# A list scheduler that models two DMA queues and chooses orders by their mean end over late transfers, in a tuned 8-core hybrid block

## The chip, the cores and the metric

The kernel runs on all 8 cores of one Trainium2 chip, as one launch. Each core takes 4096 of the 32768 tokens. The cores don't exchange data, so the time of a run is the span of its slowest core, in microseconds of device time. There is a slower state, in which the cores of one die show a lower granted TensorE clock and the run is some per cent longer.

## The reference, cut to what matters

```python
h = rmsnorm(x, norm1_g)
p = h @ w_in                              # B, C, x~ (512 each) | u, v (512 each)
y_a = b_gate * causal_depthwise_conv(c_gate * xc, conv_w)
y_b = u * (spatial_gating(layernorm(v), w_s) + b_s)     # 128x128 per head, masked
y = concat([rmsnorm(y_a, g_conv), rmsnorm(y_b, g_gmlp)])
x = x + y @ w_out
a = relu(rmsnorm(x, norm2_g) @ w_up)
x = x + (a * a) @ w_down
return rmsnorm(x, final_g)
```

Here D is 1024 and the hidden width 4096. Each core works through 8 tiles of 512 tokens. The first stage (everything up to `y @ w_out`) takes the tiles one by one. After it comes the channel mixer, in four groups of two tiles.

## The kernel before

The program is not written in the order in which it runs. Every instruction is recorded as an operation with its inputs, and a list scheduler places the operations on five in-order queues: TensorE, ScalarE, VectorE, the gpsimd queue and the sync queue. The last two only issue transfers here, apart from little else. The order that it finds is fixed in the program. In the traces read here each queue keeps that order and waits for what hasn't arrived (8.60 us on ScalarE in the case told below).

```python
def schedule(self, phys, rounds=8):
    ...
    for _ in range(rounds + 1):
        order = self.place([op for op, _ in base], phys)   # forward: times in a model
        est = max(o.finish for o in order)
        if best is None or est < best[0]:
            best = (est, order, ...)
        self.push(order, est)                              # backward: new keys
```

In `place` a transfer is modelled by one queue that serves all transfers one after the other, whoever issues them:

```python
if op.dma_key is not None:
    dma_free = max(dma_free, st + op.occ) + op.nbytes / dma_rate     # 290e3 bytes per us
    op.finish = dma_free + dma_lat + op.margin                       # dma_lat = 2.0
else:
    op.finish = st + op.dur - op.occ + occ
```

`rstd` turns a sum of squares into the factor of a norm by a logarithm and an exponential, both on ScalarE. `stats` squares a tile in four quarters, on ScalarE too. The loads at the start are chained: each weight load (gpsimd queue, casting from f32) and each quarter of a tile (sync queue) is issued only when the load three places earlier in the list has landed.

```python
def rstd(out_ap, bank, n, writes, in_ap=None, reads=None):
    act(out_ap, bank[:, 0:n] ..., AF.Ln, ...)
    act(out_ap, out_ap, AF.Exp, writes, writes, n=n, scale=-0.5)

def stats(src, q, n, ones, rows=2, first=False):
    for j in range(0, n, 2):
        act(q[:, j:j + 2, :], src[:, j:j + 2, :], AF.Square, ...)
    ...

def wload(dst, src, keys, name, nbytes):
    landed = [("landed",) + name]
    dma("pool", dst, src, gate[-3], keys + landed, ("w",) + name, nbytes, key=first())
    gate.append(landed)
...
for k in (0, 4):
    wload(WU[:, k:k + 4, :], ...)           # two loads of 1 MB
for j in range(2):
    wload(WO[:, 4 * j:4 * j + 4, :], ...)   # two loads of 2 MB
load_x(2, gate)                             # third tile: X_72, four quarters of 512 KB
```

The third tile is called X_72 in the trace; its squares are XQ_80. The norm factors are the tiles RS_77 and RS_79, the normalised branches YN, and the output weights WO. PREP are two buffers in which the weights of the channel mixer are combined, RING the six slots that hold them in use, and RA and RB the residual with the result. `load_w` combines some of the down slots in the ring itself:

```python
def load_w(n):
    s, i = wslot(), plan[n]
    if n < 32 and 16 <= i < 24:
        combine(RING[s], ws(i), wdn_d, ...)    # loads f32 from wdn, adds, stores
    else:
        dma("sp", RING[s][:, :, :, :], ws(i), ...)
```

Of the kernel before, what the change touches and what calls it, by code (L numbers as in the profile page):

```python
# [23 lines left out]
KB = 1024  # L24

ENGS = ("pe", "act", "dve", "pool", "sp")


class Op:
# [6 lines left out]
class Bank:  # L36


    def __init__(self, log):
        self.ops, self.left, self.phys = [], 0, None  # L40
        log.append(self)
# [20 lines left out]

def real(x):
    return x.ap() if isinstance(x, Late) else x


class Sched:
# [41 lines left out]
        self.ops.append(op)  # L109
        return op  # L110

    def schedule(self, phys, rounds=8):


        base = [(op, op.deps) for op in self.ops]
        best = None
        for _ in range(rounds + 1):
            for op, deps in base:
                op.deps = deps
                for b in op.banks:  # L120
                    b.left = len(b.ops)
            order = self.place([op for op, _ in base], phys)
            est = max(o.finish for o in order)
            if best is None or est < best[0]:
                best = (est, order, [(o, o.deps) for o in order],
                        [(o.opens, o.opens.phys) for o in order if o.opens is not None],
                        {o: (o.start, o.finish) for o in order})
            self.push(order, est)
        self.est_total, self.ops = best[:2]
        for o, deps in best[2]:  # L130
            o.deps = deps
            o.start, o.finish = best[4][o]
        for b, p in best[3]:
            b.phys = p
        self.by_eng = {e: [o for o in self.ops if o.eng == e] for e in ENGS}

    def push(self, order, est, lat=0.12, dma_lat=2.0, dma_rate=290e3):

        left = {o: 0 for o in order}
        for o in order:  # L140
            o.late = est
            for d in o.deps:
                left[d] += 1
        ready = {e: [] for e in ENGS}
        for o in order:
            if not left[o]:
                ready[o.eng].append(o)
        t_free = {e: est for e in ENGS}
        dma_free = est

        def dur(o):
            return o.dur if o.dma_key is None else o.occ + o.nbytes / dma_rate + dma_lat + 2 * o.margin
        while True:
            best = None
            for e in ENGS:
                if not ready[e]:
                    continue
                horizon = min(t_free[e], max(o.late - dur(o) + o.occ for o in ready[e]))
                o = max((o for o in ready[e] if o.late - dur(o) + o.occ >= horizon), key=lambda o: (o.start, o.idx))
                if best is None or (horizon, o.idx) > best[0]:  # L160
                    best = ((horizon, o.idx), o)
            if best is None:
                return
            (end, _), o = best
            ready[o.eng].remove(o)
            if o.dma_key is not None:
                dma_free = min(dma_free, o.late - dma_lat - 2 * o.margin) - o.nbytes / dma_rate
                end = min(end, dma_free)
            t_free[o.eng] = end - o.occ
            if not o.fixed:  # L170
                o.key = t_free[o.eng]
            for d in o.deps:
                d.late = min(d.late, t_free[o.eng] - lat)
                left[d] -= 1
                if not left[d]:
                    ready[d.eng].append(d)

    def place(self, ops, phys, lat=0.12, dma_lat=2.0, dma_rate=290e3):
        free = [[t, 0.0, []] for t in phys]
        for op in ops:  # L180
            op.succs = []
            op.npred = len(op.deps)
            op.ready_t = 0.0
        for op in ops:
            for d in op.deps:
                d.succs.append(op)
        ready = {e: [] for e in ENGS}
        for op in ops:
            if op.npred == 0:
                ready[op.eng].append(op)  # L190
        t_free = {e: 0.0 for e in ENGS}
        dma_free = 0.0
        cold = 3.4
        order = []
        while True:
            best = None
            for e in ENGS:
                lst = ready[e]
                if not lst:
                    continue  # L200
                soon = min((f[1] for f in free), default=1e9)

                def ready_at(o):
                    return o.ready_t if o.opens is None else max(o.ready_t, soon)
                horizon = max(t_free[e], min(ready_at(o) for o in lst))
                if horizon >= 1e9:
                    continue
                op = min((o for o in lst if ready_at(o) <= horizon), key=lambda o: (o.key, o.idx))
                if best is None or (horizon, op.idx) < best[0]:
                    best = ((horizon, op.idx), op)  # L210
            if best is None:
                break
            (st, _), op = best
            ready[op.eng].remove(op)
            if op.opens is not None:
                f = min(free, key=lambda f: f[1])
                free.remove(f)
                op.opens.phys = f[0]
                op.deps = op.deps + f[2]
            op.start = st  # L220
            occ = op.occ
            if op.eng == "pe":

                if st - t_free["pe"] > 3.0:
                    cold = 3.4
                if cold > 0:
                    occ *= 2
                    cold -= occ
            t_free[op.eng] = st + occ
            if op.dma_key is not None:  # L230
                dma_free = max(dma_free, st + op.occ) + op.nbytes / dma_rate
                op.finish = dma_free + dma_lat + op.margin
            else:
                op.finish = st + op.dur - op.occ + occ
            order.append(op)
            for b in op.banks:
                b.left -= 1
                if b.left == 0:
                    last = [o for o in b.ops if o.eng != "pe"]
                    free.append([b.phys, max(o.finish for o in b.ops) + lat, last])  # L240
            for sc in op.succs:
                sc.npred -= 1
                sc.ready_t = max(sc.ready_t, op.finish + lat)
                if sc.npred == 0:
                    ready[sc.eng].append(sc)
        assert len(order) == len(ops)
        return order

    def resolve(self):
# [70 lines left out]
def build_program():  # L320
    nc = bass.Bass("TRN2", target_bir_lowering=False)
    S = Sched()
# [21 lines left out]
    with es:  # L344
        base = (nc.sbuf_base + 1023) // 1024 * 1024
# [14 lines left out]
        o = 6  # L360
# [54 lines left out]
        banks = []  # L415
# [13 lines left out]
        def act(out, in_, func, reads, writes, n=MT, **kw):  # L429
            aps = sum(1 for v in kw.values() if not isinstance(v, (int, float)))  # L430
            S.add("act", lambda e: e.activation(out=out, in_=real(in_), func=func, **kw), reads=reads, writes=writes,  # L431
                  occ=(n / 1.2 + 200 + 70 * aps) / 1000, banks=[in_.bank] if isinstance(in_, Late) else [])

        def dve(fn, reads, writes, n=MT, rate=1, src=None):
            S.add("dve", fn, reads=reads, writes=writes, occ=(n / rate + 151) / 960,
                  banks=[src.bank] if isinstance(src, Late) else [])

        def tt(out, in0, in1, op, reads, writes, n=MT, rate=1):
            dve(lambda e: e.tensor_tensor(out=out, in0=real(in0), in1=in1, op=op), reads, writes, n, rate, in0)  # L439
# [176 lines left out]
        def ws(i):  # L616
            return ws_d[i].rearrange("p (a k n) -> p a k n", a=7, k=4)

        def prep(i, n):
            combine(PREP[n % 2], ws(i), wup_d if i < 16 else wdn_d, (i, ("pl", n % 2), ("ps", n % 2)), WO.keys(4) if n < 2 else [], 5.0)  # L620
# [7 lines left out]
        def wslot():  # L628
            return nxt("ring", RG)

        def load_w(n):
            s, i = wslot(), plan[n]
            if n < 32 and 16 <= i < 24:
                combine(RING[s], ws(i), wdn_d, (i, ("fl", s), ("fs", s)), [], 5.0)
            else:
                dma("sp", RING[s][:, :, :, :], ws(i), [("ws", i)], RING[s].keys(0, 7), ("wl", s), 2 * 128 * 3584,
                    margin=2.0)
            return s
# [258 lines left out]
        def prep_some(m):  # L897
            if m >= 1 and pos["prep"] < 24:
                n = pos["prep"]
                prep(n if n < 16 else n + 8, n)  # L900
                pos["prep"] += 1

        pos["prep"] = 0
# [165 lines left out]
```

## Time and profile before

The three runs that came with the kernel have a median of 1244.42 us (1244.34 to 1245.89).

| before, profiled run | core 7 (slowest) | mean of 8 cores |
|---|---|---|
| span | 1244.9 us | 1240.0 us |
| first product of the first convolution | 18.9 us | 18.0 us |
| TensorE's wait for YN at the first output projection | 0.0 us | 0.0 us |
| last product of the channel mixer ends | 1227.9 us | 1223.3 us |
| from there to the end | 17.0 us | 16.7 us |

The first fence is from the page of the profile, core 7: its first line, the busy times of the engines, and the shares of the chain that ended last, by engine and by line.

```profile
span 1244.9 us, 18564 instructions; the slowest of 8 cores (1235.7 to 1244.9 us)
PE 1209.6 (97%) x5880; PEld 548.5 (44%) x5880; DVE 893.4 (72%) x1377; ACT 530.4 (43%) x905; POOL 86.0 (7%) x146
PE 93%; DMA 5%; DVE 1%; issue 0%; SPq 0%; DVEq 0%; POOLq 0%
PE PS L424 93%; DMA WSB_109<-bsf 2%; DMA X_74<-xT 1%; DMA X_73<-xT 1%; DMA WV<-wv 1%; DMA WCXB_53<-wcxb 1%; DVE RA L439 0%; DVE RB L439 0%; SPq L450 0%; DVE WU L446 0%; DVEq L344 0%; DVE FSQ_102 L439 0%; DVE FSQ_101 L439 0%; DVE Z L439 0%; DVEq L284 0%
```

The second is one line of the chain of waits in order of time, same core. Its columns are start, length, and what held the chain.

```profile
68.66 1158.35 PE PS L424 x5536
```

From 68.66 to 1227.01 us nothing but TensorE's own work is on the chain. The order of instructions holds 5468 products of 512 columns; at the 0.2157 us between two of them, and with the smaller ones, that is 1200.85 us of work (an estimate from these durations). So a core that ends its last product at 1227.9 us has lost 27.0 us over all, and the rest of its span is the tail. Part of the loss is half clock: after some waits the trace records a granted TensorE clock of 0.5 for some us, and products of 512 columns then start every 0.427 us and not every 0.2157 (33.63 us, core 7).

### The profile page before, as it was taken

What the parts mean: (1) busy time and instruction counts of PE and PEld (TensorE: products, weight loads), DVE (VectorE), ACT (ScalarE), POOL (GpSimd) and SP (SyncE); (2) the same over time, 40 slices, a digit from 0 to 9 for tenths busy, and PEclk for the clock granted to TensorE, in tenths of its full rate; (3) what the DMA queues carried; (4) which work ended last, traced back from release to release, by engine and by line L of the source; (5) the groups of instructions that cost most, each with busy time, mean ns of one, the idle gap of its engine ahead of it and who ended that gap; (6) DMA issues with size and microseconds to landing.
All of it is one profiled execution on the core that took longest, in us unless ns stands there. A gap on an engine that the chain in (4) does not pass through costs nothing.

```text
span 1244.9 us, 18564 instructions; the slowest of 8 cores (1235.7 to 1244.9 us)
## 1 busy us (share of the span) xinstructions
PE 1209.6 (97%) x5880; PEld 548.5 (44%) x5880; DVE 893.4 (72%) x1377; ACT 530.4 (43%) x905; POOL 86.0 (7%) x146
## 2 busy tenths in 40 slices
PE   5899999999999999999999999999999999999994
PEld 3444444444444444444444444444444444444442
DVE  2778687877878887658759737767846876855746
ACT  4544655536554356026127205317405406503524
POOL 0100000000001011000101200000110000110000
PEclk9899999999999999999999999999999999999998
DMA  8968688596675869975577764576984645985423
GB/s 185 171 148 232 167 228 231 148 245 175 179 220 153 279 213 207 237 266 176 169 260 228 262 212 162 211 237 177 295 272 148 216 165 182 279 271 177 149 90 135
DMA packets 55183, 253.81 MB, mean 204 GB/s; under 512 B 6192, under 2 KB 6320, under 8 KB 54832
## 3 DMA queue, kind: packets, MB, share of 16 engines
q1 hardware_dynamic: 35152, 180.27, 42.8%
q0 software_dynamic: 19936, 72.36, 25.3%
q8 instruction: 49, 0.80, 0.3%
q14 instruction: 46, 0.38, 0.1%
HBM read 211.71 MB, written 65.01 MB: 222 GB/s over the span
## 4 chain that ended last, share of the span: by engine, by line
PE 93%; DMA 5%; DVE 1%; issue 0%; SPq 0%; DVEq 0%; POOLq 0%
PE PS L424 93%; DMA WSB_109<-bsf 2%; DMA X_74<-xT 1%; DMA X_73<-xT 1%; DMA WV<-wv 1%; DMA WCXB_53<-wcxb 1%; DVE RA L439 0%; DVE RB L439 0%; SPq L450 0%; DVE WU L446 0%; DVEq L344 0%; DVE FSQ_102 L439 0%; DVE FSQ_101 L439 0%; DVE Z L439 0%; DVEq L284 0%
## 5 line engine op out<-in xcount | busy, mean ns | idle before, releaser
L439 DVE TENSOR_TENSOR RB<-PS,RB 128x512 f32<-128x512 f32 x128 | 87.4, 690 | 91.4 <-PE PS L424 88.9
L424 PE MATMUL PS<-YN,WO 128*128 128x512 f16 x512 | 113.8, 379 | 0.0
L439 DVE TENSOR_TENSOR RA<-PS,RA 128x512 f32<-128x512 f32 x96 | 66.1, 690 | 60.6 <-PE PS L424 59.2
L439 DVE TENSOR_TENSOR A_89<-A_89 128x512 bf16<-128x512 bf16 (+1 forms) x192 | 94.5, 508 | 8.2 <-ACT A_89 L431 3.6
L431 ACT ACTIVATE SN_92<-PS 128x512 f32<-128x512 f32 x63 | 37.4, 595 | 106.5 <-PE PS L424 104.7
L424 PEld LDWEIGHTS PS<-YN,WO 128*128 128x128 f16 x512 | 50.1, 98 | 60.4
L424 PE MATMUL PS<-A_89,RING_83 128*128 128x512 bf16 x308 | 76.1, 379 | 0.0
L424 PE MATMUL PS<-A_89,RING_85 128*128 128x512 bf16 x308 | 76.1, 379 | 0.0
L424 PE MATMUL PS<-A_89,RING_86 128*128 128x512 bf16 x308 | 75.8, 379 | 0.0
L424 PE MATMUL PS<-A_89,RING_84 128*128 128x512 bf16 x308 | 75.5, 379 | 0.0
L424 PE MATMUL PS<-H_96,RING_87 128*128 128x512 f16 x308 | 75.1, 379 | 0.0
L424 PE MATMUL PS<-H_96,RING_83 128*128 128x512 f16 x308 | 74.5, 379 | 0.0
L424 PE MATMUL PS<-H_96,RING_88 128*128 128x512 f16 x308 | 74.3, 379 | 0.0
L424 PE MATMUL PS<-H_96,RING_84 128*128 128x512 f16 x308 | 74.3, 379 | 0.0
L431 ACT ACTIVATE SN_90<-PS 128x512 f32<-128x512 f32 x66 | 39.2, 595 | 76.7 <-PE PS L424 75.6
L424 PE MATMUL PS<-A_89,RING_88 128*128 128x512 bf16 x280 | 69.4, 379 | 0.0
L424 PE MATMUL PS<-A_89,RING_87 128*128 128x512 bf16 x280 | 69.1, 379 | 0.0
L431 ACT ACTIVATE SN_93<-PS 128x512 f32<-128x512 f32 x64 | 38.2, 596 | 71.8 <-PE PS L424 71.3
L424 PE MATMUL PS<-H_96,RING_85 128*128 128x512 f16 x280 | 67.9, 379 | 0.0
L424 PE MATMUL PS<-H_96,RING_86 128*128 128x512 f16 x280 | 67.4, 379 | 0.0
L431 ACT ACTIVATE SN_91<-PS 128x512 f32<-128x512 f32 x63 | 37.5, 595 | 70.1 <-PE PS L424 68.0
L439 DVE TENSOR_TENSOR SN_92<-PS,SN_92 128x512 f32<-128x512 f32 x63 | 43.4, 690 | 27.4 <-PE PS L424 22.7
(231 smaller groups left out, 2029.2 us busy)
## 6 DMA issues: line engine op xcount, KB each, us to landing
RING_83<-ws_s SPq DMA_DIRECT2D x21, 896.0 KB, 6.0
RING_84<-ws_s SPq DMA_DIRECT2D x21, 896.0 KB, 6.4
RING_87<-ws_s SPq DMA_DIRECT2D x20, 896.0 KB, 5.3
RING_88<-ws_s SPq DMA_DIRECT2D x20, 896.0 KB, 6.2
RING_85<-ws_s SPq DMA_DIRECT2D x19, 896.0 KB, 6.0
RING_86<-ws_s SPq DMA_DIRECT2D x19, 896.0 KB, 6.3
ws_s<-PREP_65 SPq DMA_DIRECT2D x12, 896.0 KB, 6.3
ws_s<-PREP_66 SPq DMA_DIRECT2D x12, 896.0 KB, 5.6
```

The source lines that it names most:

```text
L424: ins = e.matmul(real(o_), lhsT=l, rhs=r, start=st, stop=sp, skip_group_check=True)
L431: S.add("act", lambda e: e.activation(out=out, in_=real(in_), func=func, **kw), reads=reads, writes=writes, occ=(n / 1.2 + 200 + 70 * aps) ...
L439: dve(lambda e: e.tensor_tensor(out=out, in0=real(in0), in1=in1, op=op), reads, writes, n, rate, in0)
```

## The change

The intent is to let the scheduler see the chip better, and to take an order that bears late transfers. There are four main parts: two DMA queues that share one rate, half each when both are busy; a search of 60 random tries that keeps the order with the lowest mean end over six draws of late transfers, in place of the lowest end without any; new intervals for ScalarE and VectorE; and in the first group the down slots 24 to 31 combined in the ring in place of 16 to 23. Cut to its core:

```diff
+DMA_FIRST, DMA_LAT = 2.3, {"sp": 2.0, "act": 2.0, "pool": 3.5}
+class Queues:
+    def __init__(self, rate=300e3): ...
+    def issue(self, eng, t, nbytes):
+        left, other = self.left, "pool" if eng == "sp" else "sp"
+        ...
+            busy = [q for q in left if left[q] > 0]
+            step = min(dt, min(left[q] for q in busy) * len(busy))
+            for q in busy:
+                left[q] -= step / len(busy)
+        ...
+        left[eng] += nbytes
+        mine, his = left[eng], left[other]
+        return self.t + (2 * mine if mine <= his else mine + his) / self.rate + DMA_LAT[eng]
...
-    def schedule(self, phys, rounds=8):
+    def schedule(self, phys, rounds=8, tries=60):
+        draws = [{op: rnd.choice((0.0, 0.0, 0.0, 1.0)) * rnd.uniform(1.0, 8.0) * (not op.fixed) for op in dmas} for _ in range(6)]
+        for t in range(tries + 1):
+            if t:
+                for o, k in best[5].items():
+                    o.key = k if o.fixed else k + rnd.gauss(0, 0.3)
...
-                if best is None or est < best[0]:
+                goal = sum(self.replay(order, d) for d in draws) / len(draws)
+                if best is None or goal < best[0]:
...
-                dma_free = max(dma_free, st + op.occ) + op.nbytes / dma_rate
-                op.finish = dma_free + dma_lat + op.margin
+                op.finish = queues.issue(op.eng, st + op.occ, op.nbytes) + op.margin
...
-                  occ=(n / 1.2 + 200 + 70 * aps) / 1000, ...
+                  occ=(n / 1.2 + 70 + 70 * aps) / 1000, dur=(n / 1.2 + 290 + 70 * aps) / 1000,
...
-            if n < 32 and 16 <= i < 24:
+            if n < 32 and i >= 24:
                 combine(RING[s], ws(i), wdn_d, ...)
...
-                prep(n if n < 16 else n + 8, n)
+                prep(n, n)
```

Left out are a rule by which the scheduler holds back three of the eight PSUM banks (the buffers that TensorE writes to), the separate 3.5 us for a landing on the gpsimd queue in the backward pass, and the bookkeeping of the search. No product, no byte and no instruction of arithmetic is added or removed. Only orders move, and which slots are combined where.

More of the change, by code (lines that the diff above doesn't have):

```diff
@@ L1 @@
 import contextlib
+import random
 import numpy as np
@@ L64, in real, with __init__ @@
     return x.ap() if isinstance(x, Late) else x
+class Queues:
+    def __init__(self, rate=300e3):
+        self.rate, self.t, self.left = rate, DMA_FIRST, {"sp": 0.0, "pool": 0.0}
+    def issue(self, eng, t, nbytes):
+        left, other = self.left, "pool" if eng == "sp" else "sp"
+        dt, self.t = max(0.0, t - self.t) * self.rate, max(self.t, t)
+        while dt > 0 and (left["sp"] > 0 or left["pool"] > 0):
+            busy = [q for q in left if left[q] > 0]
+            step = min(dt, min(left[q] for q in busy) * len(busy))
+            for q in busy:
+                left[q] -= step / len(busy)
+            for q in busy:
+                if left[q] < 1:
+                    left[q] = 0.0
+            dt -= step
+        left[eng] += nbytes
+        mine, his = left[eng], left[other]
+        return self.t + (2 * mine if mine <= his else mine + his) / self.rate + DMA_LAT[eng]
 class Sched:
@@ L110, in add @@
         return op
-    def schedule(self, phys, rounds=8):
+    def schedule(self, phys, rounds=8, tries=60):
         base = [(op, op.deps) for op in self.ops]
+        rnd = random.Random(1)
+        dmas = [op for op, _ in base if op.dma_key is not None]
+        draws = [{op: rnd.choice((0.0, 0.0, 0.0, 1.0)) * rnd.uniform(1.0, 8.0) * (not op.fixed) for op in dmas} for _ in range(6)]
         best = None
-        for _ in range(rounds + 1):
-            for op, deps in base:
-                op.deps = deps
-                for b in op.banks:
-                    b.left = len(b.ops)
-            order = self.place([op for op, _ in base], phys)
-            est = max(o.finish for o in order)
-            if best is None or est < best[0]:
-                best = (est, order, [(o, o.deps) for o in order],
-                        [(o.opens, o.opens.phys) for o in order if o.opens is not None],
-                        {o: (o.start, o.finish) for o in order})
-            self.push(order, est)
-        self.est_total, self.ops = best[:2]
+        for t in range(tries + 1):
+            if t:
+                for o, k in best[5].items():
+                    o.key = k if o.fixed else k + rnd.gauss(0, 0.3)
+            for _ in range(3 if t else rounds + 1):
+                for op, deps in base:
+                    op.deps = deps
+                    for b in op.banks:
+                        b.left = len(b.ops)
+                keys = {op: op.key for op, _ in base}
+                order = self.place([op for op, _ in base], phys)
+                if len(order) < len(base):
+                    break
+                est = max(o.finish for o in order)
+                times = {o: (o.start, o.finish) for o in order}
+                goal = sum(self.replay(order, d) for d in draws) / len(draws)
+                if best is None or goal < best[0]:
+                    best = (goal, order, [(o, o.deps) for o in order],
+                            [(o.opens, o.opens.phys) for o in order if o.opens is not None], times, keys, est)
+                for o in order:
+                    o.start, o.finish = times[o]
+                self.push(order, est)
+        self.goal, self.ops, self.est_total = best[0], best[1], best[6]
         for o, deps in best[2]:
@@ L135, in schedule, with replay, push @@
         self.by_eng = {e: [o for o in self.ops if o.eng == e] for e in ENGS}
-    def push(self, order, est, lat=0.12, dma_lat=2.0, dma_rate=290e3):
+    def replay(self, order, late, lat=0.12):
+        t_free = {e: 0.0 for e in ENGS}
+        queues, cold, end = Queues(), 3.4, 0.0
+        for o in order:
+            st = t_free[o.eng]
+            for d in o.deps:
+                if d.finish + lat > st:
+                    st = d.finish + lat
+            occ = o.occ
+            if o.eng == "pe":
+                if st - t_free["pe"] > 3.0:
+                    cold = 3.4
+                if cold > 0:
+                    occ *= 2
+                    cold -= occ
+            t_free[o.eng] = st + occ
+            if o.dma_key is not None:
+                o.finish = queues.issue(o.eng, st + o.occ, o.nbytes) + late[o]
+            else:
+                o.finish = st + o.dur - o.occ + occ
+            o.start = st
+            if o.finish > end:
+                end = o.finish
+        return end
+    def push(self, order, est, lat=0.12, dma_rate=290e3):
         left = {o: 0 for o in order}
@@ L151, in dur @@
         def dur(o):
-            return o.dur if o.dma_key is None else o.occ + o.nbytes / dma_rate + dma_lat + 2 * o.margin
+            return o.dur if o.dma_key is None else o.occ + o.nbytes / dma_rate + DMA_LAT[o.eng] + 2 * o.margin
         while True:
@@ L166, in push @@
             if o.dma_key is not None:
-                dma_free = min(dma_free, o.late - dma_lat - 2 * o.margin) - o.nbytes / dma_rate
+                dma_free = min(dma_free, o.late - DMA_LAT[o.eng] - 2 * o.margin) - o.nbytes / dma_rate
                 end = min(end, dma_free)
@@ L176, in push, with place @@
                     ready[d.eng].append(d)
-    def place(self, ops, phys, lat=0.12, dma_lat=2.0, dma_rate=290e3):
+    def place(self, ops, phys, lat=0.12):
         free = [[t, 0.0, []] for t in phys]
@@ L191, in place @@
         t_free = {e: 0.0 for e in ENGS}
-        dma_free = 0.0
+        queues = Queues()
         cold = 3.4
         order = []
+        unopened = [o.idx for o in ops if o.opens is not None]
+        reserve = 3
         while True:
@@ L203, in ready_at @@
                 def ready_at(o):
-                    return o.ready_t if o.opens is None else max(o.ready_t, soon)
+                    if o.opens is None:
+                        return o.ready_t
+                    if len(free) <= reserve and o.idx > unopened[min(3, len(unopened) - 1)]:
+                        return 1e9
+                    return max(o.ready_t, soon)
                 horizon = max(t_free[e], min(ready_at(o) for o in lst))
@@ L218, in place @@
                 op.opens.phys = f[0]
+                unopened.remove(op.idx)
                 op.deps = op.deps + f[2]
@@ L245, in place @@
                     ready[sc.eng].append(sc)
-        assert len(order) == len(ops)
         return order
@@ L431, in act @@
             S.add("act", lambda e: e.activation(out=out, in_=real(in_), func=func, **kw), reads=reads, writes=writes,
-                  occ=(n / 1.2 + 200 + 70 * aps) / 1000, banks=[in_.bank] if isinstance(in_, Late) else [])
+                  occ=(n / 1.2 + 70 + 70 * aps) / 1000, dur=(n / 1.2 + 290 + 70 * aps) / 1000,
+                  banks=[in_.bank] if isinstance(in_, Late) else [])
         def dve(fn, reads, writes, n=MT, rate=1, src=None):
-            S.add("dve", fn, reads=reads, writes=writes, occ=(n / rate + 151) / 960,
-                  banks=[src.bank] if isinstance(src, Late) else [])
+            S.add("dve", fn, reads=reads, writes=writes, occ=(n / rate + 65) / 960,
+                  dur=(n / rate + 237) / 960, banks=[src.bank] if isinstance(src, Late) else [])
         def tt(out, in0, in1, op, reads, writes, n=MT, rate=1):
```

## The prediction

> **What bounds the kernel now.** TensorE. On the slowest core (7, 1244.9 us) the page has it busy 97%, and the chain of waits gives it one unbroken stretch from 68.7 to 1227.0 us. The instruction order holds 5468 matmuls of 512 columns; at 0.2157 us each (timeline) plus the small ones that is 1200.9 us, an estimate from trace durations, of which 1157 us lie behind 68.7. That stretch has no slack. [...] All that can be lost or won is about 27 us before 68.7 (late loads, and the half clock after a wait: after 2.9 us idle, 16 matmuls took 6.0 us, not 3.45) and 17 us behind the last product. On the other cores the waits look the same; core 0 alone also loses 2.6 us on a down slot combined in the ring. A gain of 2% would need 25 of these 44 us.
>
> **What the change does.** Work and bytes stay; orders and the choice of the eight ring-combined down slots move.
> 1. Ring-combined slots go from the first half of group 0, where the gpsimd queue also loads 4 MB of residual, to its second half. That should remove core 0's 2.6 us and add no wait: a slot's load took 6 to 16 us, its use is two down units (24 us) off.
> 2. The tail's order is nearly the same: within 0.5 us.
> 3. The start changes. TensorE has the second tile's first statistics ahead of the first convolution: its input came at 21.9 us (ScalarE timeline), so that convolution moves from 18.95 to about 22.2, on a cold clock. Tile 1's normalise comes about 1 us later and is now used first, at about 35.1 instead of 33.6 us, again cold. The bias product moves ahead by 5.3 us of TensorE work. Its input (spatial weights, cast and masked) was ready at 60.4 us, because three 256 KB loads on the sync queue took 10 to 20 us beside the weight loads; "DMA: Bandwidth & Descriptors" (Queues, rings and completion order) has each engine alternating between queues, and the trace agrees: they landed at 55, 59, 66 us. I expect a wait of about 3 us there and a cold clock after it. In return the wait on WU (2.0 us and 1.7 us cold) goes.
> 4. On the gpsimd queue WCXB1's second half moves behind WV's first, WCXB3's second half behind WU's first, about 3 us later each; the engines are saturated there (DMA share 0.96 to 1.03), so little follows.
>
> **Sum.** On core 7 TensorE is then about 3 us behind, on cores 2 and 5 about 5, on core 0 about 2 (estimates from these event times). The slowest core comes to 1245 to 1248. Against that, the scheduler's intervals for VectorE and ScalarE now fit the trace better (128x512 f32 adds start every 0.61 us), and its choice tolerates late transfers. I set 1245.
>
> **What would show it.** Unbroken TensorE from about 70 to 1227 us: step 1. Waits of the second tile's statistics near 18 to 22 us, of its convolution at 35, of the bias product near 57 to 60: step 3. No wait on a RING tile on any core. If the bias wait is missing, expect 1240 or so.
>
> **What would make it wrong.** Spatial weights landing earlier (faster by up to 6 us); a late slot in group 0's second half, or a head-of-line wait on the gpsimd queue (slower by 5 to 20 us).
>
> Predicted 1245 us, 8 in 10 between 1238 and 1251; faster by over 2%: 0.01, within 2%: 0.97, slower: 0.02.

## More of the kernel before

```profile
82.73 0.69 ACT L431 ACTIVATE RS_79<-PS,SMALL 128x512 f32<-128x512 f32 x1 [1.97 <-PE PS L424]
83.31 1.05 ACT L431 ACTIVATE XQ_80<-X_72 128x1024 bf16<-128x1024 f32 x1
84.26 0.62 ACT L431 ACTIVATE RS_79<-RS_79 128x512 f32<-128x512 f32 x1
```

Even here a square of the third tile stands between the logarithm and the exponential of the first branch. Its quarter had landed at 73.77 us, so the square ran at once, and the exponential came 0.95 us later than it might have. No wait of TensorE follows from it: the first product on YN has none in its timeline.

## The result, and the profile after

Ratios here and below are of the mean of one kernel's fast runs to the mean of the other's in the same rounds. Executions in which one die ran at a lower clock are left out of the means. The plain ratio of the means of all listed fast runs differs from them by up to 0.0004, the ratio of the medians by more.

| | before | after |
|---|---|---|
| fast runs | 1243.37, 1244.34, 1244.42, 1245.89 us | 1253.49, 1256.89, 1257.31 us |
| slow runs | none in these rounds | 1285.12, 1426.29 us |
| ratio of fast runs | | 1.0092, 95% interval 1.0067 to 1.0116 |

The changed kernel is about 11 us slower, above the upper end of the predicted range (1251). The profiled run is a fast one. First the page, core 2, which is now the slowest:

```profile
span 1255.7 us, 18545 instructions; the slowest of 8 cores (1242.8 to 1255.7 us)
PE 1209.8 (96%) x5880; PEld 548.6 (44%) x5880; DVE 894.0 (71%) x1377; ACT 528.4 (42%) x905; POOL 85.5 (7%) x146
PE 90%; DMA 7%; DVE 1%; issue 1%; DVEq 0%; ACT 0%; SPq 0%; POOLq 0%; ACTq 0%
PE PS L497 90%; DMA X_72<-xT 2%; DMA WU<-wu 1%; DMA WCXB_52<-wcxb 1%; DMA X_74<-xT 1%; DMA WV<-wv 1%; DMA X_73<-xT 1%; DMA WCXB_54<-wcxb 1%; DVE RB L513 0%; DMA WCXB_51<-wcxb 0%; DVE RA L513 0%; DVE YN L513 0%; DVE H_96 L516 0%; DVEq L417 0%; DVE FSQ_102 L513 0%
```

The work is the same, and the busy time of TensorE too. But X_72, the third tile, is now first among the transfers on the chain, where it was not before. The chain of waits in order of time shows how it got there:

```profile
49.82 10.76 DMA WU<-wu
60.64 13.93 DMA X_72<-xT
74.64 11.94 DMA X_72<-xT
...
87.62 0.62 ACT RS_79 L504
88.33 2.37 DVE YN L513 x2
...
90.84 302.13 PE PS L497 x1532
```

TensorE's unbroken stretch starts only at 90.84 us in place of 68.66. ScalarE's timeline of the same core answers to the one shown of before (core 7; start, length, instruction):

```profile
77.38 0.67 ACT L504 ACTIVATE RS_79<-PS,SMALL 128x512 f32<-128x512 f32 x1
86.66 1.06 ACT L504 ACTIVATE XQ_80<-X_72 128x1024 bf16<-128x1024 f32 x1 [8.60 <-DMA X_72<-xT]
87.62 0.61 ACT L504 ACTIVATE RS_79<-RS_79 128x512 f32<-128x512 f32 x1
```

And the groups of TensorE's waits on that core (what it waited for: us in total, times, the longest):

```profile
PE PS L497 <- ACT XQ_80 L504: 8.8, 2, 8.1
PE PS L497 <- DVE YN L513: 7.9, 1, 7.9
PE PS L497 <- ACT XQ_81 L504: 5.9, 2, 5.8
PE PS L497 <- DVE FSQ_102 L513: 3.5, 1, 3.5
PE PS L497 <- DVE HT_64 L513: 2.7, 1, 2.7
```

The logarithm of the first branch is done at 78.1 us. Behind it in ScalarE's order stands the square of quarter 3 of the third tile, which has to wait for its load until 86.6 us. Behind that stands the exponential, which has had its input all the while. VectorE waits for the exponential and TensorE for VectorE: 7.88 us. TensorE's timeline around its first product on YN, before (core 7) and after (core 2):

```profile
86.78 4.05 PE L424 MATMUL PS<-HT_64,WCXB_52 128*128 128x512 f16 x18
90.67 1.03 PE L424 MATMUL PS<-YN,WO 128*128 128x512 f16 x4
...
80.63 2.32 PE L497 MATMUL PS<-WV,HT_64 128*128 128x512 f16 x10
90.84 7.40 PE L497 MATMUL PS<-YN,WO 128*128 128x512 f16 x21 [7.88 <-DVE YN L513]
```

TensorE's own order has a part in this: before, 18 products of the second tile's convolution (3.9 us) stand between the last on WV and the first on YN, and after none. No run moves them alone. The Trainium skill says in "PSUM — Partial Sum Buffer" (Engine vs sequencer instructions) that the queues of ScalarE, VectorE and GpSimdE are strict FIFO, and the trace agrees: no later instruction of ScalarE ran in those 8.60 us.

Before, the same quarter 3 landed at 79.84 us, on core 7. Two things make it late on core 2 after. The sync queue now issues the quarters in the order 0, 3, 2, 1. Quarter 3 waits for the landing of quarter 0 (its gate in the chained list), and 1 and 2 stand behind it although their gates have opened, so three of the four are issued together, from 74.64 us on. And by then the first two PREP loads have been issued, at 72.48 and 73.00 us, in place of 82.06 and 82.58. The three quarters took 11.9 to 12.8 us beside them. The first PREP load on the gpsimd queue and the landing times of the four quarters, before (core 7) and after (core 2):

```profile
82.06 0.53 POOL L450 DMA_DIRECT2D PREP_65<-wup  x1 [24.07 <-DVE SQ_62 L439]
DMA to landing us min/median/max: 3.8/6.3/13.6
...
72.48 0.53 POOL L524 DMA_DIRECT2D PREP_65<-wup  x1 [14.20 <-DVE WO L520]
DMA to landing us min/median/max: 11.9/12.8/13.9
```

All 8 cores show it: the wait for YN is 3.7 to 7.9 us, where it was 0.0 on all 8 before. The table gives means over the cores, read from TensorE's timeline. "Rest" is the time lost up to the last product (its end less 1200.85 us) that is not idle time, so mostly half clock. The traces of cores 2 and 4 of before and of 0 and 6 of after lack 67 or 68 product records each. The gaps that this leaves, some 3.2 us on each of these cores, count as idle in the fourth row and are missing from "rest", by the same amount before and after.

| mean of 8 cores, us | before | after | difference |
|---|---|---|---|
| idle before the first convolution | 8.8 | 13.3 | +4.5 |
| idle from there to 110 us, without YN | 7.5 | 3.6 | -3.9 |
| wait for YN at the first output projection | 0.0 | 5.6 | +5.6 |
| idle from 110 us to the last product | 1.3 | 1.6 | +0.3 |
| rest | 4.9 | 6.5 | +1.6 |
| tail behind the last product | 16.7 | 17.2 | +0.5 |
| span | 1240.0 | 1248.6 | +8.6 |

The first two rows are the start that the prediction was busy with, and they nearly cancel. What remains is the wait for YN and the colder clock after it. That clock shows in the 64 products behind the wait: they took 16.68 us in all on core 2, and 14.20 us on the same core in the first experiment below, where nothing waits.

The slowest core has something more. On core 2 the tail is 20.4 us, 3.4 us longer than on core 7 of before, and not by the order: VectorE's last instruction ends 10.4 us behind the last product there and 10.3 us on core 7 of before. The last four stores took 8.5 to 9.6 us to land, in place of 6.0 to 6.4. Such long landings stand in the traces where two neighbouring cores (0 and 1, 2 and 3, and so on) take nearly the same time, each counted from its own start: in the three pairs whose last VectorE instructions end within 0.8 us of each other (after and experiments 3 and 9) the slowest store took 8.4 to 9.9 us; in the three pairs of run 10 that end 8 to 13 us apart it took 3.6 to 4.9. One pair 3.2 us apart (experiment 6) took 9.6 too. That the stores of the two meet at the end is a reading; no run tests it, and the traces don't show how the cores' starts lie to each other.

### The profile page after: what moved, and what is told of

It is laid out like the page before. It is cut to its first block, busy times and chain, and to the rows that moved or that the text cites. A ratio compares the mean times of both kernels' runs of the same rounds, so it can differ in the third digit from the quotient of the medians.

```text
span 1255.7 us, 18545 instructions; the slowest of 8 cores (1242.8 to 1255.7 us)
## 1 busy us (share of the span) xinstructions
PE 1209.8 (96%) x5880; PEld 548.6 (44%) x5880; DVE 894.0 (71%) x1377; ACT 528.4 (42%) x905; POOL 85.5 (7%) x146
## 4 chain that ended last, share of the span: by engine, by line
PE 90%; DMA 7%; DVE 1%; issue 1%; DVEq 0%; ACT 0%; SPq 0%; POOLq 0%; ACTq 0%
PE PS L497 90%; DMA X_72<-xT 2%; DMA WU<-wu 1%; DMA WCXB_52<-wcxb 1%; DMA X_74<-xT 1%; DMA WV<-wv 1%; DMA X_73<-xT 1%; DMA WCXB_54<-wcxb 1%; DVE RB L513 0%; DMA WCXB_51<-wcxb 0%; DVE RA L513 0%; DVE YN L513 0%; DVE H_96 L516 0%; DVEq L417 0%; DVE FSQ_102 L513 0%
## 5 line engine op out<-in xcount | busy, mean ns | idle before, releaser
L513 DVE TENSOR_TENSOR A_89<-A_89 128x512 bf16<-128x512 bf16 (+1 forms) x192 | 95.2, 510 | 20.6 <-ACT A_89 L504 15.4
```

What stands on the lines that cost most here:

```text
L513: dve(lambda e: e.tensor_tensor(out=out, in0=real(in0), in1=in1, op=op), reads, writes, n, rate, in0)
```

## The experiments

Theory A is the one just told: ScalarE's order puts a square with a late input between the logarithm and the exponential. It has a part about the order and a part about the lateness, and the first three runs take one or the other away. The rivals are that the loss comes from what else the change moved, at the start, in the ring or behind; each text gives the numbers by which they differ. A second question, put afterwards, is which part of the change is to blame for that order.

The first four ran on one chip with before at 1245.35 us (1243.28 to 1246.75, 7 runs, all fast).

**1. The one square moved behind the exponential.** Kernel after, ScalarE's order only:

```diff
+        move(at("act", ("sq", 2, 3)), at("act", ("sq", 2, 2)))   # just before the next square
```

> The changed kernel with one ScalarE instruction moved: the square of the third tile's last input quarter, which stood between the logarithm and the exponential of the first tile's norm, goes behind that tile's other norm, just before the next square. Theory A (in the changed kernel that square waits for a late input load and holds up the exponential, so the normalised YN and the first output projection come late): the wait of TensorE for YN, 3.7 to 7.9 us by core, falls below 1.5 us and the cold clock after it goes; slowest core 1245 to 1249 us instead of 1253 to 1257. Rival B (the moved down slots cost) and rival C (the new order of the first 60 us costs): nothing they need is touched, so 1253 to 1257.

Measured: 1248.69 us (1245.4 to 1251.05, 4 runs), ratio 1.0022 (1.0002 to 1.0042). The wait for YN is 0.0 on all 8 cores. These are lines of the timeline of TensorE, core 2:

```profile
77.91 2.32 PE L498 MATMUL PS<-WV,HT 128*128 128x512 f16 x10
80.07 14.20 PE L498 MATMUL PS<-YN,WO 128*128 128x512 f16 x64
94.11 4.26 PE L498 MATMUL PS<-HT,WCXB 128*128 128x512 f16 x19
```

One instruction moved by a few places takes back 7.1 of the 8.6 us of the mean span in the profiled run (1241.4 us), of which 1.8 us are a shorter tail (15.4 us). Over all fast runs it is 6.1 us of 8.7, and by the ratios about three quarters of the loss of the slowest core. Theory A holds for most of the cost. It doesn't come all the way back to before: cores 3 and 7, now the slowest at 1246.3 and 1246.9 us, wait 4.4 us near 923 us. The groups of waits of core 3:

```profile
PE PS L498 <- ACT XQ L505: 12.8, 5, 7.8
PE PS L498 <- DVE RB L514: 4.4, 1, 4.4
```

VectorE was held there by residual loads (7.32 us for RA at 922.27 us in its timeline).

**2. The quarters issued in turn.** Kernel after, with the four loads in the order 0, 1, 2, 3 on the sync queue, and their squares in that order on ScalarE:

```diff
+        in_turn("sp", [("xl", 0, j) for j in range(4)])
+        in_turn("act", [("sq", 2, j) for j in range(4)])
```

> The changed kernel with the third tile's four quarter loads issued in their old order 0 1 2 3 on the sync queue (the change issues 0 3 2 1, and 3 waits for 0 to land), and the four squares in that order; a square still stands between logarithm and exponential. Theory A, with the lateness made on the sync queue: the second quarter is issued near 67 us instead of 74.6 and lands by 80 instead of 85 to 87, the YN wait falls below 2 us, slowest core 1245 to 1250. If the place of the square alone is what costs, the wait stays at 4 to 8 us and the time at 1253 to 1257. Rivals B and C: 1253 to 1257.

Measured: 1256.55 us (1253.31 to 1257.85, 4 runs), ratio 1.0083 (1.0065 to 1.0102). The wait for YN is 3.7 to 7.7 us. My expectation missed: the quarters did not land earlier. On core 7 quarter 1 was issued at 73.97 us, because its gate is WO's first half, and that landed at 73.91 us: the gpsimd queue now issues the two halves of WO in the other order (53.67 and 56.62 us). The three quarters landed from 83.91 to 86.42 us, beside PREP again. So the swapped quarters are not a cause by themselves. The swap of WO's halves, which the prediction passed over, held them as late in this run; no run puts WO's halves back.

**3. The PREP loads kept behind the third tile.** Kernel after, with the first two PREP loads made to wait for the landing of the four quarters; order of the quarters and of the squares as in after:

```diff
+        for n in range(2):
+            op = at("pool", ("pl", n))
+            op.deps = op.deps + [at("sp", ("xl", 0, j)) for j in range(4)]
```

> The changed kernel with the first two weight preparation loads (512 KB each landed, on the gpsimd queue) held until the third tile's four quarters have landed; in the changed kernel they start at 72.5 us, in the kernel before at 78.5 to 82 us. If these loads are what makes the quarters slow (11 to 13 us to land, against 4 to 8 before), the awaited quarter lands near 79 to 81 us, the YN wait falls to 0 to 3 us and the slowest core to 1246 to 1252. If the late issue alone is at fault, the wait stays above 4 us and the time at 1253 to 1257.

Measured: 1248.35 us median of 4 runs, of which one (1271.0) is slow; ratio of the fast runs 1.0016 (0.9999 to 1.0033). The profile fell in a slow run, so only its six cores with an undisturbed clock are read. The wait for YN there is 0.0 to 2.6 us. On core 0 three quarters were issued at 70.81 to 71.96 us and landed 3.8 to 5.1 us later, where beside PREP it was 11.9 to 12.8 (core 2 of after). Over the six cores these three took 3.8 to 7.0 us, and over the eight cores of after 7.4 to 13.1. So the lateness needs the PREP loads beside the quarters. Order and lateness are both needed, as the kernel before shows from the other side: there a square stood between the two as well, with its data long there.

**4. The slots alone.** Kernel before, with the two lines of the diff that choose the slots:

```diff
-            if n < 32 and 16 <= i < 24:
+            if n < 32 and i >= 24:
-                prep(n if n < 16 else n + 8, n)
+                prep(n, n)
```

> The kernel before with the slots alone changed (down slots 24 to 31 combined in the ring, 0 to 23 prepared); the scheduler is the old one and orders of the first 300 us stay as they were. Theory A: within 2 us of the kernel before, 1242 to 1247, no YN wait, and no wait on a RING tile on core 0. Rival B: 1250 or more, with waits on RING tiles in the second half of group 0 (about 560 to 660 us).

Measured: 1245.05 us (1243.99 to 1246.82), ratio 0.9996 (0.9979 to 1.0013). No wait for YN. The slots cost nothing and bring nothing: core 0 has lost its wait of 2.6 us for a ring slot, but cores 2 and 7 have one of 3.4 and 2.7 us near 494 us. The slots alone do not move the time.

These four leave open which part of the change makes the order, and what the late waits of experiment 1 are. Theory D: those waits come from the new order of the gpsimd queue. Theory E: the queue model, with half the rate for each queue, makes the order that loses. Theory F: the random search with its goal does. Theory G: no share models two queues well enough. The next four ran together, with before at 1245.37 us (1243.61 to 1247.6 in its six fast runs, and one slow).

**5. The gpsimd queue's order of before, later on.** Experiment 1, and from the first output store on the order of loads and stores on the gpsimd queue copied from before:

```diff
+ORDER = """s00 r00 s10 r10 s01 s11 r01 r11 s02 s12 ... r13"""   # stores, residual loads, tile loads
+        mine = mine[[o.tag[0] for o in mine].index("os"):]
+        for i, k in zip(where, ORDER.split()):
+            S.ops[i] = ...                                        # the operation that k names
```

> Kernel after with the square moved (as in e1) and, from the first output store on, the gpsimd queue's order of loads and stores taken from the kernel before. e1 left a wait of 4.4 us at 923.7 us on cores 3 and 7 for a late residual load. Theory D (that wait comes from the new order of the gpsimd queue in the later groups): the wait near 923 us goes, no TensorE wait over 2 us after 100 us on any core, slowest core 1241 to 1246, ratio 0.996 to 1.001 against before. Rival (the wait comes from TensorE running ahead of what the queue can carry, whatever the order): a wait of 3 us or more stays, ratio 1.001 to 1.004.

Measured: fast runs 1252.71 to 1257.69, ratio 1.0078 (1.005 to 1.0106). Theory D is wrong: six of the eight cores wait 4.4 to 5.7 us between 915 and 930 us. That is the rival's wait, but the loss is larger than the rival gave (1.001 to 1.004). The waits for the residual grew: core 4 now has 10.6 us of them in four pieces.

```profile
PE PS L504 <- DVE RB L520: 10.6, 4, 4.4
PE PS L504 <- DVE HT L520: 7.8, 2, 5.2
PE PS L504 <- ACT XQ L511: 7.4, 1, 7.4
```

Cores 1 and 7 have none over 0.8 us and end at 1237.4 and 1238.4 us. My reading, which no run tests, is that a gpsimd order that fits one VectorE order does not fit another; why some cores wait at 920 us and others don't stays open.

**6. No random search.** Kernel after with `tries=0` in place of 60: queue model, goal and intervals stay.

> Kernel after with no tries of the random search (only the repeated placing that before also had, but still with the two-queue model and the goal over late transfers). Its ScalarE order has logarithm and exponential of the first branch together, but two squares of the third tile still stand before the second branch's pair. Theory E (the half-rate queue model is at fault, and the random search only picked the place): TensorE still waits 2 us or more near 80 to 90 us for a normalised branch, 1249 to 1256. Rival F (the search with its goal made the loss): no such wait over 1 us, 1241 to 1247.

Measured: 1256.28 us (1255.11 to 1262.22), ratio 1.0096 (1.0064 to 1.0127). The order has the first branch's pair together, but the loss is the same as the change's. The products on YN in the timeline of core 3, the slowest:

```profile
82.05 2.75 PE L497 MATMUL PS<-YN,WO 128*128 128x512 f16 x12 [1.97 <-DVE YN L513]
87.43 1.86 PE L497 MATMUL PS<-YN,WO 128*128 128x512 f16 x4 [2.63 <-ACT RS L504]
90.99 4.28 PE L497 MATMUL PS<-YN,WO 128*128 128x512 f16 x13 [1.70 <-DVE YN L513]
```

ScalarE had idled 6.69 us for the load of X before a square at 84.47 us. So the search picks the place where the queue is held, but without it the queue is held too. The waits on YN add up to 3.9 to 6.3 us on six cores, 0.6 us on core 0 and none on core 4. Rival F, that the search made the loss, falls (the goal was still in this run).

**7. The old queue model, all else of the change kept.**

```diff
-        left, other = self.left, "pool" if eng == "sp" else "sp"
-        ...
+        self.t = max(self.t, t) + nbytes / 290e3
+        return self.t + 2.0
```

> Kernel after with the queue model alone put back to the old one queue (290 KB per us, one transfer after the other, 2.0 us more), search and goal kept. The order it finds issues the third tile's quarters in turn and has logarithm and exponential before any of their squares. Theory E (queue model): the wait for the normalised branch at 80 to 91 us is under 1.5 us on all cores, 1239 to 1248, ratio 0.995 to 1.003. Rival F (search and goal): the wait stays at 3 us or more, 1250 to 1258.

Measured: fast runs 1249.03, 1256.3 and 1258.9, ratio 1.0074 (1.0027 to 1.012). Here I was right on the mechanism and wrong on the time. The wait for YN is 0.0 on all cores, the first convolution starts at 16.5 to 19.0 us, and cores 3, 4 and 7 end at 1236.3 to 1237.8. But the slowest, core 1, loses 12.9 us to residual waits from 635 us on:

```profile
PE PS L485 <- DVE RB L501: 12.9, 5, 3.9
PE PS L485 <- ACT XQ L492: 9.4, 3, 8.3
```

The wait at 90 us comes with the new queue model. The later waits don't need it, since the model here is the old one.

**8. The two-queue model with the measured share.** What the model says can be set beside what came. The change's scheduler expects quarter 0 of the third tile from 59.7 to 66.3 us and quarter 3 from 66.4 to 73.0, in its own schedule. On core 2 they came from 60.64 to 74.57 and from 74.64 to 86.57. It gives each queue half of 300 KB per us. From 61 to 74 us, with loads of WO and of the quarter under way at once, the records of core 2 show 136 KB per us written by the gpsimd queue, which casts f32 to 16 bit, so about 272 KB per us read, and 40 KB per us moved by the sync queue: 40 of 312, or 13% of the bytes read. By time, the sync queue's packets had 15% of the 16 DMA engines and the gpsimd queue's 79%. The Trainium skill ("DMA: Bandwidth & Descriptors", Queues, rings and completion order) says that each engine goes round between the queues it has work for, a packet at a time. The trace agrees with the direction, for the gpsimd queue's packets wrote 7282 bytes on average (so read 14.6 KB), and the sync queue's 3693. But packets in strict turn aren't the whole of it as the profile counts them: in those 13 us there were 243 packets of the gpsimd queue and 142 of the sync queue. Whether the profile's packet is the page's, no run shows. The share isn't one number either: from 75 to 86.5 us, beside the PREP loads, the sync queue moved 84 KB per us and the gpsimd queue wrote 91 (182 read), so 32% of the bytes read were the sync queue's. The model was mended with the first share, for both:

```diff
+CAST = ("w", "pl", "fl")              # the casting loads of the gpsimd queue
+    def share(self, q):
+        if self.left[other] <= 0:
+            return self.rate
+        sync = 0.15 if self.cast else 0.5
+        return self.rate * (sync if q == "sp" else 1 - sync)
```

> Kernel after with the two-queue model kept, but the sync queue given 0.15 of the rate while the gpsimd queue has a casting weight load under way, in place of half (from the trace of after: 0.13 of the bytes read, 0.15 of the time). Search and goal kept. Its own schedule then says 58.4 to 73.8 us for the first quarter of the third tile, where the chip had 60.2 to 73.8 in before. Theory E, the share is the wrong number: no wait over 1.5 us for the normalised branch, 1238 to 1246, ratio 0.994 to 1.001. Rival G (two queues cannot be modelled by a share, so the order found is no better than the change's): a wait of 3 us or more somewhere before 100 us, over 1250.

Measured: 1246.32 us (1245.23 to 1250.07, 4 runs, all fast), ratio 1.0016 (0.999 to 1.0042). The wait for YN is gone on every core but one (0.3 us on core 3). The groups of waits on core 2 have no YN:

```profile
PE PS L509 <- DVE WCXB L532: 8.8, 3, 3.3
PE PS L509 <- ACT XQ L516: 7.5, 2, 7.3
PE PS L509 <- DVE FSQ L525: 3.3, 1, 3.3
```

The share alone, half or 0.15, turns 1.0092 into 1.0016, some 9 us. Theory E holds for the wait; the time and the ratio lie just above what it gave (1246 and 1.001). One rival is left: each model was searched once, with one seed, so an order can also be good or bad by chance. Both orders found with half the rate (after and 6) wait for YN at the first output projection, and none of those found otherwise (7, 8, 9 and 10) does by more than 0.3 us; no run changes the seed. That the change with the right share is faster than before, which my range allowed, doesn't show.

**9 to 11. Can the parts be had together?** Experiment 7 had the better start and 8 the quieter middle. Run 9 uses the old queue for transfers issued in the first 100 us of modelled time and the model of 8 after them; run 10 does so for 60 us; run 11 is 8 again, in five rounds.

```diff
+START = 100.0                          # 60.0 in run 10
+        if t < START:
+            self.one = max(self.one, t) + nbytes / 290e3
+            return self.one + 2.0
```

> A try for a kernel that beats before: the queue model of e8 (sync queue 0.15 beside casting loads), but transfers issued in the first 100 us of the modelled time go by the old one queue. Reason: e7 (one queue throughout) had its first convolution product at 16.5 to 19.0 us against 20.0 to 23.8 in e8, and lost its time in waits after 100 us (up to 13.4 us on core 1), of which e8 had at most 4.7. If the two stages can be had apart: first convolution product before 20 us, no wait over 1.5 us for a normalised branch, waits after 100 us under 5 us in sum, slowest core 1238 to 1244, ratio 0.993 to 0.999. If the later waits come back with the early start (cores that get ahead wait for the same late loads): 1246 to 1254.

> As e9 with the switch of models at 60 us, before the third tile is loaded and the first branch normalised. Its order puts one square of the third tile between the two pairs of logarithm and exponential. If the gain of the early start is had by 60 us: as e9, 1238 to 1245; it differs from e9 by under 3 us unless the square between the pairs waits again (then a TensorE wait of 2 us or more near 85 us).

> e8 unchanged, in 5 rounds beside e9 and e10, since its first ratio (1.0016, 0.999 to 1.0042) left open whether it is faster or slower than before. Theory (the change's search is worth nothing here even with the right share): ratio 0.999 to 1.003. Rival (with the right share it pays): under 0.998.

| fast runs, against before at 1242.49 to 1248.74 us (10 fast runs) | range | ratio |
|---|---|---|
| 9 (100 us) | 1247.88 to 1250.43 us, 5 runs | 1.0031 (1.0017 to 1.0045) |
| 10 (60 us) | 1247.43 to 1250.96 us, 5 runs | 1.0030 (1.0013 to 1.0047) |
| 11 (8 again) | 1244.67 to 1250.92 us, 6 runs | 1.0017 (0.9998 to 1.0036) |

Each had one slow run besides, and before had one. Neither hope came true. The early start is there: in run 10 the first convolution starts at 18.0 us in the mean of the cores (as in before; 21.4 in run 11), and the fastest core ends at 1233.1 us, below any of before's profiled run (1235.7), though with a tail of 14.4 us where that had 16.1 at the least. But cores 0 and 6, at 1245.5 and 1246.7 us, wait 5.0 and 5.3 us after 110 us, in several waits of up to 2.9 us, where no core of run 11 waits over 0.7 us (small gaps of 3.2 us on cores 0 and 6 of both runs, where some 65 product records are missing, are left out). In run 9 the slowest cores, 0 and 1, wait only 3.3 and 0.8 us after 110 us; their tails are 20.4 and 19.3 us, with last stores that took up to 9.7 us. The metric is the slowest of eight, and the mean span of the cores is no better either: 1241.0 us over the five fast runs of run 10, 1240.2 over those of before. No version that I tried is faster than the kernel before.

## Why the prediction was wrong

- **The bound was read rightly.** TensorE's work is the same in every run, and no order could win more than the 44 us around it. The predicted class, within 2%, holds (1.0092); the range doesn't. That the class holds is no credit to the path, since the 11 us that were lost are not in the prediction's sum.
- **Step 1, the slots: no new wait as predicted in the profile of after, and no gain.** Experiment 4 gives 0.9996. The 2.6 us on core 0 went, but core 0 was not the slowest, and 3.4 and 2.7 us came on others in that run.
- **Step 2, the tail: right for the order and the mean, not for the slowest core.** The mean tail went from 16.7 to 17.2 us; the wait for FSQ_102 from 2.8 to 3.5. On core 2 the last stores added 3.4 us.
- **Step 3, the start: the moves were right, the balance a little too dark.** The first convolution came at 23.9 us on core 7 (predicted 22.2, before 18.9). The wait for HT_64 came at 35.6 us (predicted 35.1). The wait on WU is gone. The bias wait of "about 3 us" is not there: 0.5 us at most, since the spatial weights landed at 51.30, 54.76 and 58.93 us on core 7 in place of 55.14, 58.95 and 66.08. TensorE's idle time up to 110 us, without YN, went on core 7 from 19.0 to 16.7 us, where the prediction had it 3 us behind. For the missing bias wait it said "expect 1240 or so". That case came and 1240 did not: the early part was won, and lost again at YN.
- **Step 4 is the one that failed:** "so little follows". The prediction looked at two swapped halves of the convolution weights and stopped at about 68 us, where the chain of before turned to pure TensorE. It took the stretch behind for safe ("That stretch has no slack" was taken to mean that nothing new would hold it up). The swaps further on were in the new order too and were not followed: WO's halves, the quarters of the third tile, and the PREP loads ten microseconds earlier. Together with a square in front of an exponential they cost 3.7 to 7.9 us of waiting on every core, and about 1.6 us of clock in the mean. The prediction's own sign, "Unbroken TensorE from about 70 to 1227 us", is missing: on core 2 the unbroken stretch starts at 90.84 us.
- **The sum's last sentence failed too:** the choice "tolerates late transfers". It draws delays of 1 to 8 us for a quarter of the transfers. But the quarter that mattered was 13.6 us later than its own model had it (86.57 against 73.0), because the model gave the sync queue half the rate and the chip gave it about 13% while quarter 0 came and 32% while quarter 3 did: it was issued 8.2 us later than in the model and then took 11.9 us in place of 6.6. Experiments 6 and 7 put it on the queue model, and 8 on the share.
- **Among the reasons for being wrong** it had named "a head-of-line wait on the gpsimd queue (slower by 5 to 20 us)". The size was right and the queue was another: the wait came at the head of ScalarE's queue, and of the sync queue.

Four things stay open: why the residual loads hold some cores near 635 and 920 us in experiments 1, 5 and 7, where 8 has one such wait (2.5 us at 1108 us, core 3); why the same kernel's cores differ by 10 us; what makes the last stores slow on some pairs of cores; and what the new intervals, the goal and the reserve of banks do by themselves, which no run took apart.

## What to carry to other kernels

When a diff changes a scheduler, follow every engine's order past the point where the chain of the old kernel becomes pure compute: look for an instruction whose input is a load, standing ahead of one that the bounding engine needs, and ask when that load lands in the new order of both queues. Such an instruction is harmless while its data are early, as in before, and costs most of its lateness when they aren't (on core 2 the exponential came 9.5 us later than it might have, and TensorE lost 7.9). A scheduler that scores its own orders is as good as its transfer model, so set its times for a few transfers beside the trace before its robustness is trusted. And where the time is the slowest of several cores, look at the slowest ones to their end: run 10 started 3.4 us earlier than run 11 in the mean and was no faster, for two of its cores waited later.

## What the Trainium skill lacked or had wrong

- "DMA: Bandwidth & Descriptors" (Queues, rings and completion order) has the engines alternate by packet, but gives no share for a casting gpsimd load beside a plain sync load. Here it was 272 KB per us read against 40 beside WO, with 79% and 15% of the engines' time, and 182 against 84 beside PREP, with 59% and 37%.
- The same page doesn't say how a load slows beside such traffic in terms of landing time: 512 KB in 3.8 us with no weight load beside it (the first of three quarters in experiment 3, core 0) and 11.9 to 13.9 us beside weight loads (after).
- "TensorE: Matmul & The Clock Gate" (What's actually happening) has the half clock after an idle window of about 3.4 us, and calls the window free-running. The records of the granted clock agree with the length: in before, core 7, it went to half at 69.25 us and back at 72.66, 3.41 us later. But the wait before that was only 2.03 us (it ended at 68.66), with TensorE busy on both sides of it, while in after, core 2, a wait of 2.75 us (it ended at 36.24) left the clock at full. The section has no rule for a window that is idle in part.
- No page has a word on how far the eight cores of one program drift apart: 1235.7 to 1244.9 us in one fast run of before, with equal work.
